# A scheduling planner gets measured lengths, a two-engine reservation and a new order of weight slabs

## The chip, the cores and the metric

The kernel runs on one core of one Trainium2 chip, in one launch. The metric is the device time in microseconds (us) of that core. Five engines share the work and run at their own pace: PE (TensorE: matmuls and transposes), DVE (VectorE), ACT (ScalarE), POOL (GpSimd) and SP (SyncE), whose queue issues every DMA of this kernel. Each engine carries out its own list of instructions in order. Semaphores hold an instruction back until what it reads has been written, and until what it overwrites has been read.

## The reference

One layer of a bidirectional encoder on 512 tokens of width 1024, all in float32:

```
h   = rms_norm(x)
all = h @ w_in          # attention q,k,v,gate az; delta q,k,v (dq,dk,dv), beta, decay, gate dz; merge gates gA,gB
A   = softmax(rope(norm(q)) rope(norm(k))^T / sqrt(128)) v          # 8 heads, 2 kv heads
y_att = (A * silu(az)) @ w_br_att
qkv = silu(short_conv(dq,dk,dv))                                    # depthwise, 5 taps
o   = gated delta rule over qkv, chunk by chunk, forward + backward  # needs (I + L)^-1 per chunk, head, direction
y_dn = (rms_norm(o) * silu(dz)) @ w_br_dn
mix = (sigmoid(gA) * y_att + sigmoid(gB) * y_dn) @ w_out
x   = x + rms_norm(mix)
x   = x + rms_norm(sigmoid(x @ w_ple_gate) * (p @ w_ple_proj))
```

## The kernel before, in words

**Products.** Each float32 product is made from three PE passes. A matrix is split into a rounded part `hi` and a rest `lo`, and lo x hi, hi x lo and hi x hi are added up in one PSUM bank (lines 434 to 436 in `gemm_t`, 451 to 453 in `gemm_n`, 469 to 471 in `gemm_k`). The weights come as *slabs* of 1024 x 128 (512 KB), 72 of them: dq, dk, dv, dz, az, gA, gB, ydn (the branch projection of the delta rule) and yatt (that of attention), eight each. A slab takes eight steps of three matmuls, 128 x 512. The other weights (kv, q0, q1, out0, out1, pg0, pg1) come in blocks of the same size in bytes. `fetch` (line 377) issues the DMA of each into one of two `wraw` buffers. `loader` (392) has `split` (192) make the two parts: ACT casts `whi`, and then DVE or POOL subtracts to give `wlo`.

**What hangs on a slab.** dq, dk and dv go through `conv_tail` (678): one ACT pass, four DVE taps that read PSUM, a tanh on ACT, a DVE product, four PE transposes, and one more DVE pass. The gates dz, az, gA and gB go through `gate_tail` (482): tanh on ACT, one DVE product for dz and az and none for gA and gB, and a DMA to DRAM, from where they are read back later.

**The delta rule** runs for two groups of four heads. `phase_a` (759) makes the masked products kk and qk, inverts 32 x 32 triangles on DVE and combines them to 128 x 128 on PE. The inversion is here called the *chain*: 30 steps that depend on one another, each of a product (833) and a subtraction (835), both with two operands in SBUF. `phase_b` (939) is the scan over chunks. Group 1 starts when group 0 has been scanned. `phase_y` (1041) normalises and gates the result. `att_head` (1261) does the attention of one head; `yatt_job` (1399), `out_job` (1477) and `pg_job` (1537) finish the layer.

**The planner.** The order of the instructions on every engine is made while the program is built, by `Flow` (line 33). Each part of the kernel is a generator. Flow keeps a clock `now`, and a list of busy intervals for each engine. `op` (66) finds the first free place of a given length on one engine and books it; all instructions are put out in the order of their planned starts. ("pe", cost) moves the clock on by the planned length of some matmuls. Nothing of these times reaches the chip: only the order does, and there the semaphores decide when each instruction starts. `V`, `A` and `G` (151 to 158) book DVE, ACT and POOL; `Q` (160) books the issue of a DMA, and so the order on SP's queue. `ORDER` (126) lists the slabs and blocks, `OUT0` tells before which slabs the four blocks of out0 are fetched, `PR` gives the priorities of parts (a lower number goes first), and `GAP` a pause between bursts of small matmuls. `split` puts the subtraction of a slab on POOL where that ends less than 1.5 us (of planned time) later than on DVE.

```
    def fit(self, eng, dur, t):                    # line 57
...
        while i < len(busy) and busy[i][0] < t + dur:
            t = max(t, busy[i][1])
...
        for m in range(30, 0, -1):                 # line 837, the chain
            t = V(0.25 + 2 * m * (31 - m) * 0.00108, t - 0.1, step, m)
```

Of the kernel before, what the change touches and what calls it, by code (L numbers as in the profile page):

```python
# [34 lines left out]
class Flow:  # L35
    """Interleaves the kernel's parts (generators) into one instruction order.

    A part yields ("pe", cost) behind matrix instructions, ("at", t) and ("ev", event) to wait,
    ("get", tag) to take a tile slot; the first part in priority that can go on is traced next.
    Instructions of the other engines are traced in the order of their planned starts.  # L40
    """
# [97 lines left out]
W1 = 0  # L139


@with_exitstack
def layer(ctx, tc, x, p, wt, wba, wn, wpp, npre, rows, qkn, hd16, npost, pnorm, dnorm, cs, out):
# [43 lines left out]
    def either(dep, *ways):  # L187
        """the way that ends first"""
        w = min((F.fit(w[0], w[1], max(F.now + 0.2, dep + 0.15))[0] + w[1], i, w) for i, w in enumerate(ways))[2]
        return op(w[0], w[1], dep, *w[2:])  # L190

    def split(src, hi, lo, dep, n, sbuf=False, slow=False):
# [8 lines left out]
        fn = (dve if eng == "DVE" else pool).tensor_sub  # L201
        t2 = op(eng, n * (0.00113 if eng == "DVE" else 0.00228), t, fn, lo, src, hi.bitcast(F32))
# [43 lines left out]
    def rsqrt(n, dep, s, mul, eps, post=1.0, src=None):  # L246
        """s = post (mul src + eps)^-1/2, n elements in each partition; src is s if not given"""
# [175 lines left out]
    def gemm_t(name, mh=hh, ml=hl, need=None):  # L423
        """need: events by k"""
# [6 lines left out]
        for k in range(8):  # L431
# [8 lines left out]
            yield "pe", 0.648  # L440
        return o

    def gemm_n(name, t, sh, sl_):
        yield "get", "mm"
        o = bank("mm")
        for k in range(8):
# [7 lines left out]
            yield "pe", 0.648  # L454
        return o

    def gemm_k(name, sh, sl_):
        """the four token tiles at once, so that the weights pass through"""
# [4 lines left out]
        for k in range(8):  # L463
            yield "ev", slab["blk", name, k // 2][0]
            hi, lo = (w[:, k % 2, :] for w in slab["blk", name, k // 2][1])
            for t in range(NT):
# [73 lines left out]
    # e^c, e^(clast - c), e^clast; each [dir, chunk, head]  # L540
# [1138 lines left out]
```

## Time and profile before

| | |
|---|---|
| median of 3 runs | 802.01 us (801.99 to 803.83) |
| the profiled execution: first to last instruction | 802.0 us |
| PE busy | 770.2 us, 96% |
| DVE busy | 517.7 us, 65% |
| POOL busy | 363.3 us, 45% |
| ACT busy | 316.8 us, 39% |
| mean granted clock of TensorE | 0.983 of full speed |
| DMA | 96.70 MB, mean 121 GB/s |

Busy time is the union of the intervals in which an engine had an instruction under way. The granted clock is given as a share of 2.4 GHz: 1.00 is 2.4 GHz and 0.50 is 1.2 GHz, and a value between them is a mean over a stretch that holds both. The span and the median agree, so that stretches of the trace can be set directly against the measured time. Many lines of the trace have the number L89: this is where Flow puts out booked instructions, so they are told apart by the names of their tiles.

### The profile page before, as it was taken

What the parts mean: (1) busy time and instruction counts of PE and PEld (TensorE: products, weight loads), DVE (VectorE), ACT (ScalarE), POOL (GpSimd) and SP (SyncE); (2) the same over time, 40 slices, a digit from 0 to 9 for tenths busy, and PEclk for the clock granted to TensorE, in tenths of its full rate; (3) what the DMA queues carried; (4) which work ended last, traced back from release to release, by engine and by line L of the source; (5) the groups of instructions that cost most, each with busy time, mean ns of one, the idle gap of its engine ahead of it and who ended that gap; (6) DMA issues with size and microseconds to landing.
All of it is one profiled execution on the core that took longest, in us unless ns stands there. A gap on an engine that the chain in (4) does not pass through costs nothing.

```text
span 802.0 us, 11761 instructions
## 1 busy us (share of the span) xinstructions
PE 770.2 (96%) x4522; PEld 636.1 (79%) x4522; DVE 517.7 (65%) x904; ACT 316.8 (39%) x522; POOL 363.3 (45%) x303
## 2 busy tenths in 40 slices
PE   8999999898999999996999999999999999989995
PEld 6787888686789987884779988887888888878884
DVE  4577788998845599996556554618677644523634
ACT  6465433325342144322434133424666533331421
POOL 6354574243521277443332116845465554461421
PEclk9999999998999999998899999999999999999999
DMA  6463226226211263525313116334144346643213
GB/s 247 131 198 107 79 92 158 84 87 158 66 55 40 92 197 115 150 92 153 130 54 105 40 53 190 104 120 132 66 157 132 119 141 217 225 137 133 87 45 131
DMA packets 52970, 96.70 MB, mean 121 GB/s; under 512 B 20849, under 2 KB 22449, under 8 KB 52914
## 3 DMA queue, kind: packets, MB, share of 16 engines
q1 hardware_dynamic: 52914, 95.95, 37.9%
q8 instruction: 35, 0.57, 0.3%
q14 instruction: 21, 0.17, 0.1%
HBM read 79.12 MB, written 16.81 MB: 120 GB/s over the span
## 4 chain that ended last, share of the span: by engine, by line
PE 73%; DVE 17%; DMA 3%; issue 2%; ACT 2%; POOL 2%; SPq 0%; POOLq 0%; DVEq 0%; ACTq 0%
PE mm L434 11%; PE mm L436 11%; PE mm L435 11%; DVE blk L835 4%; PE mm L451 4%; PE mm L452 4%; PE mm L453 4%; DVE u L89 3%; DVE f L89 3%; DVE blk L833 3%; PE mm L469 3%; PE mm L470 3%; PE mm L471 3%; PE aux L1007 2%; PE aux L975 2%
## 5 line engine op out<-in xcount | busy, mean ns | idle before, releaser
L89 POOL TENSOR_TENSOR wlo<-wraw,whi 128x1024 fp32r<-128x1024 f32 x71 | 170.5, 2402 | 259.9 <-ACT whi L89 241.8
L434 PE MATMUL mm<-u,wlo 128*128 128x512 f32 x576 | 236.5, 411 | 4.8 <-POOL wlo L89 4.6
L436 PE MATMUL mm<-u,whi 128*128 128x512 f32 x576 | 227.0, 394 | 0.0
L435 PE MATMUL mm<-u,whi 128*128 128x512 f32 x576 | 226.8, 394 | 0.0
L434 PEld LDWEIGHTS mm<-u,wlo 128*128 128x128 f32 x576 | 109.6, 190 | 26.6 <-POOL wlo L89 5.6
L436 PEld LDWEIGHTS mm<-u,whi 128*128 128x128 f32 x576 | 109.5, 190 | 24.1
L435 PEld LDWEIGHTS mm<-u,whi 128*128 128x128 f32 x576 | 109.9, 191 | 19.7
L89 ACT CAST whi<-wraw 128x1024 fp32r<-128x1024 f32 x84 | 87.9, 1046 | 67.9 <-PE mm L471 28.3
L89 DVE SCALAR_TENSOR_TENSOR f<-mm,cw,f 128x510 f32<-128x510 f32 (+1 forms) x96 | 71.7, 748 | 13.6 <-ACT f L89 10.9
L451 PE MATMUL mm<-u,u 128*128 128x512 f32 x128 | 51.4, 402 | 2.2 <-DVE u L89 2.2
L452 PE MATMUL mm<-u,u 128*128 128x512 f32 x128 | 50.6, 395 | 0.0
L453 PE MATMUL mm<-u,u 128*128 128x512 f32 x128 | 50.5, 395 | 0.0
L89 POOL TENSOR_TENSOR u<-wraw,u 128x1024 fp32r<-128x1024 f32 x15 | 36.6, 2440 | 27.7 <-ACT u L89 27.6
L89 ACT ACTIVATE f<-mm 128x512 f32<-128x512 f32 (+1 forms) x44 | 25.5, 580 | 46.7 <-PE mm L453 30.0
L469 PE MATMUL mm<-whi,u 128*128 128x512 f32 x96 | 39.8, 415 | 2.5 <-ACT whi L89 2.5
L89 ACT ACTIVATE go<-mm 128x512 f32<-128x512 f32 x32 | 19.2, 599 | 56.6 <-PE mm L436 33.2
L470 PE MATMUL mm<-wlo,u 128*128 128x512 f32 x96 | 38.6, 402 | 1.9 <-POOL wlo L89 1.9
L89 DVE TENSOR_TENSOR u<-aux,u 128x512 f32<-128x512 f32 (+1 forms) x48 | 31.9, 685 | 12.5 <-ACT u L89 10.1
L471 PE MATMUL mm<-whi,u 128*128 128x512 f32 x96 | 38.5, 401 | 0.0
L835 DVE TENSOR_TENSOR blk<-blk,blk 128x30 f32<-128x30 f32 (+14 forms) x60 | 37.0, 616 | 2.1
L89 ACT COPY c<-aux 128x512 f32<-128x512 f32 x18 | 10.6, 586 | 62.7 <-DVE f L89 39.6
L89 POOL TENSOR_TENSOR u<-f,u 128x512 fp32r<-128x512 f32 x16 | 22.4, 1402 | 19.1 <-ACT u L89 19.1
(254 smaller groups left out, 1332.9 us busy)
## 6 DMA issues: line engine op xcount, KB each, us to landing
wraw<-in_wt_dram SPq DMA_DIRECT2D x72, 512.0 KB, 3.5
wraw<-in_wn_dram SPq DMA_DIRECT2D x28, 512.0 KB, 4.1
u<-CI SPq DMA_DIRECT2D x16, 256.0 KB, 6.8
u<-in_x_dram SPq DMA_DIRECT2D x4, 512.0 KB, 8.7
eD<-c SPq DMA_DIRECT2D x8, 256.0 KB, 2.1
gate_gA<-go SPq DMA_DIRECT2D x8, 256.0 KB, 2.8
gate_dz<-go SPq DMA_DIRECT2D x8, 256.0 KB, 2.1
gate_gB<-go SPq DMA_DIRECT2D x8, 256.0 KB, 3.0
```

The source lines that it names most:

```text
L89: fn(*a, **k)
L434: pe.matmul(o, lo[:, k, :], mh(k), start=(k == 0), stop=False)
L435: pe.matmul(o, hi[:, k, :], ml(k), start=False, stop=False)
L436: pe.matmul(o, hi[:, k, :], mh(k), start=False, stop=(k == 7))
L451: pe.matmul(o, b, hi, start=(k == 0), stop=False)
L452: pe.matmul(o, a, lo, start=False, stop=False)
L453: pe.matmul(o, a, hi, start=False, stop=(k == 7))
L469: pe.matmul(o[t], b, hi, start=(k == 0), stop=False)
L470: pe.matmul(o[t], a, lo, start=False, stop=False)
L471: pe.matmul(o[t], a, hi, start=False, stop=(k == 7))
L833: dve.tensor_tensor(out=tt[:, 0:m, 0:31 - m], in0=b[:, 0:m, m:m + 1].to_broadcast(sh), in1=w[:, m:m + 1, m + 1:].to_broadcast(sh), op=ALU. ...
L835: dve.tensor_sub(w[:, 0:m, m + 1:], w[:, 0:m, m + 1:], tt[:, 0:m, 0:31 - m])
```

## The change

Lengths in the planner are replaced: the three matmuls of a step from 0.648 to 0.682, four 128-column products from 0.87 to 0.90, four scan operations on DVE from 0.92 to 1.05, a POOL subtraction from 0.00228 to 0.00232 us an element, and so on. A new booking `W` takes a place that is free on DVE and on POOL at once, and reserves both; the instruction itself still runs on DVE. W replaces V for DVE work with two operands in SBUF (the chain, the split on DVE, the SiLU product of the conv tail, the merge sums, the sandwich norm and others). While a chain is being planned (`chains[0]` above 0), `split` uses POOL only where that ends no later than DVE would (`HOT` = 0, else `COOL` = 1.5). ORDER, OUT0, PR and GAP are new. Because slabs now come in any order within their kind, jobs count their turns (`turn`) where they tested for the first or the last index. No computation, tile or buffer changes.

```diff
+    def slot(self, engs, dur, dep):
+        t = max(self.now + 0.2, dep + 0.15)
+        while True:
+            at = [self.fit(e, dur, t) for e in engs]
+            if all(a == t for a, _ in at):
+                return t, [i for _, i in at]
+            t = max(a for a, _ in at)
...
+    def W(dur, dep, fn, *a, **k):
+        return op(("DVE", "POOL"), dur, dep, fn, *a, **k)
...
-            tv = F.fit("DVE", n * 0.00113, t + 0.15)[0] + n * 0.00113
-            tp = F.fit("POOL", n * 0.00228, t + 0.15)[0] + n * 0.00228
-            if slow or tp < tv + 1.5:
+            eng = ("DVE", "POOL")
+            tv = F.slot(eng, n * 0.00113, t)[0] + n * 0.00113
+            tp = F.slot(("POOL",), n * 0.00232, t)[0] + n * 0.00232
+            if slow or tp < tv + (HOT if chains[0] else COOL):
                 eng = "POOL"
...
+        chains[0] += 1
         for m in range(30, 0, -1):
-            t = V(0.25 + 2 * m * (31 - m) * 0.00108, t - 0.1, step, m)
+            t = W(0.32 + 2 * m * (31 - m) * 0.00104, t - 0.1, step, m)
             yield "at", t - 1.0
+        chains[0] -= 1
...
-            yield "pe", 0.648
+            yield "pe", 0.682
...
 ORDER = """
-dq0 dk0 gA0 dq1 dk1 dq2 dk2 dk3 dq3 dk4 dz0 dq4 dk5 dq5 dz1 gA1
-dk6 dv0 gB0 gB1 dz2 dv1 dv2 dk7 dv3 dq6 gB2 dq7 az0 dz3 gA2 az1
-az2 dz4 gB3 dv4 dv5 dv6 az3 dz5 gB4 dz6 az4 gA3 dv7 az5 kv dz7
-gA4 gB5 gB6 gA5 az6 q0 gB7 ydn0 q1 gA6 az7 gA7 ydn1 free_h ydn2 ydn3
-ydn4 ydn5 ydn6 ydn7 vec yatt0 yatt1 yatt2 yatt3 yatt4 yatt5 yatt6 yatt7 out0 out1 pg0
+dq2 az3 dk3 dk0 dq3 dq0 dk1 dk2 dq1 dv0 dz2 gB1 dk7 dz4 dq7 dk6
+dz3 dz7 dz0 gB6 dz6 gA7 dk5 dv1 dv2 dv3 az2 dq6 dk4 dq5 dq4 az4
+gB4 gA5 dz1 dv7 dv6 gA6 az1 az0 dv5 gA4 gB7 gA1 gA0 az5 az6 dv4
+kv gA2 gA3 dz5 gB5 q0 az7 gB3 q1 ydn2 gB0 ydn6 gB2 free_h ydn3 ydn0
+ydn1 ydn5 ydn4 ydn7 yatt5 yatt6 vec yatt1 yatt4 yatt7 yatt2 yatt0 yatt3 out0 out1 pg0
 pg1
 """
-OUT0 = 'ydn3 ydn4 ydn5 yatt2'
-PR = dict(dec=9, dm1=7, y=2, conv=5, gate=9, kv=2, q=6, head=7, ple=11)
-GAP = 0.6
+OUT0 = 'ydn0 ydn4 ydn5 yatt6'
+PR = dict(dec=7, dm1=7, y=1, conv=3, gate=0, kv=5, q=7, head=1, ple=11)
+GAP = 0.0
+COOL, HOT = 1.5, 0
```

## Rows read from the trace of the kernel before

**Rows 1.** The page's first part: busy time, share of the span and number of instructions of PE, DVE and POOL.

```profile
PE 770.2 (96%) x4522; PEld 636.1 (79%) x4522; DVE 517.7 (65%) x904; ACT 316.8 (39%) x522; POOL 363.3 (45%) x303
```

**Rows 2.** The busy time of each engine by stage. Columns: the stretch in us from the start, its length, then PE, PEld (weight loads), DVE, ACT and POOL busy with their numbers of instructions, the granted clock, the share of the DMA engines, GB/s.

```profile
136.00:206.00 70.00, 63.00 (x416) 50.01 (x415) 63.22 (x105) 27.09 (x39) 25.90 (x12) 0.93 0.39 116
206.00:300.00 94.00, 93.97 (x759) 80.64 (x759) 59.40 (x122) 31.04 (x49) 37.04 (x30) 1.00 0.29 91
300.00:390.00 90.00, 80.52 (x427) 65.46 (x426) 79.06 (x127) 32.73 (x45) 43.47 (x27) 0.94 0.44 131
540.00:698.00 158.00, 157.45 (x765) 130.78 (x765) 101.00 (x191) 79.09 (x141) 83.74 (x70) 1.00 0.45 147
698.00:716.00 18.00, 15.79 (x63) 12.54 (x62) 7.61 (x7) 6.56 (x9) 10.85 (x6) 0.91 0.46 141
```

**Rows 3.** The same view for the five stretches in which TensorE had the lower granted clock behind an idle time of PE.

```profile
153.60:157.00 3.40, 3.40 (x10) 2.65 (x9) 3.26 (x6) 1.43 (x4) 2.40 (x1) 0.50 0.02 5
184.30:191.10 6.80, 5.31 (x15) 4.34 (x16) 4.21 (x6) 5.27 (x9) 2.38 (x1) 0.50 1.03 203
368.60:372.00 3.40, 3.40 (x8) 2.69 (x9) 3.02 (x13) 0.00 (x0) 0.38 (x1) 0.50 0.00 0
378.80:385.70 6.90, 4.98 (x13) 3.87 (x13) 4.60 (x7) 5.76 (x10) 1.92 (x1) 0.51 0.90 234
706.50:709.90 3.40, 3.40 (x10) 2.62 (x9) 0.60 (x1) 1.63 (x3) 2.97 (x2) 0.50 0.22 58
```

**Rows 4.** What PE waited for: us in total, how often, the longest.

```profile
PE mm L434 <- POOL wlo L89: 4.6, 2, 3.3
PE mm L666 <- DVE f L89: 3.5, 1, 3.5
PE mm L666 <- DVE u L89: 3.5, 2, 3.0
```

**Rows 5.** The timeline of POOL and of DVE in the first chain: start, duration, engine, line, operation, tiles and shapes; x4 is four instructions in one row.

```profile
138.66 2.40 POOL L89 TENSOR_TENSOR wlo<-wraw,whi 128x1024 fp32r<-128x1024 f32 x1 [3.62 <-ACT whi L89]
153.72 2.40 POOL L89 TENSOR_TENSOR wlo<-wraw,whi 128x1024 fp32r<-128x1024 f32 x1 [7.09 <-ACT whi L89]
...
138.79 2.34 DVE L833 TENSOR_TENSOR blk<-blk,blk 128x58 f32<-128x58 f32 x1
141.17 0.22 DVE L835 TENSOR_TENSOR blk<-blk,blk 128x58 f32<-128x58 f32 x1
...
153.49 3.10 DVE L89 SCALAR_TENSOR_TENSOR f<-mm,cw,f 128x510 f32<-128x510 f32 x4
```

**Rows 6.** The two chains whole (138.3 to 181.3, 335.0 to 371.8), all engines; then the products of the chain (line 833) and its subtractions (line 835) alone, DVE only, in stretches that hold one chain each.

```profile
138.30:181.30 43.00, 39.97 (x174) 32.68 (x173) 40.59 (x75) 11.99 (x17) 17.08 (x8) 0.96 0.26 89
335.00:371.80 36.80, 33.54 (x143) 27.33 (x142) 34.93 (x67) 8.37 (x11) 14.40 (x7) 0.96 0.28 93
...
136.00:184.00 48.00, 13.46 (x30) 0.96 0.32 106
333.00:373.00 40.00, 13.89 (x30) 0.96 0.27 92
...
136.00:184.00 48.00, 18.52 (x30) 0.96 0.32 106
333.00:373.00 40.00, 18.45 (x30) 0.96 0.27 92
```

**Rows 7.** Groups of instructions: engine, operation, tiles, shapes, number | busy us, mean ns of one | idle time before them. POOL's slab subtractions in the stretches 136 to 184 and 333 to 373, and the same subtraction where DVE did it, over the whole run.

```profile
L89 POOL TENSOR_TENSOR wlo<-wraw,whi 128x1024 fp32r<-128x1024 f32 x7 | 16.9, 2413 | 27.7 <-ACT whi L89 27.7
L89 POOL TENSOR_TENSOR wlo<-wraw,whi 128x1024 fp32r<-128x1024 f32 x6 | 14.6, 2432 | 23.8 <-ACT whi L89 23.8
...
L89 DVE TENSOR_TENSOR wlo<-wraw,whi 128x1024 fp32r<-128x1024 f32 x13 | 17.9, 1373 | 2.0 <-ACT whi L89 1.2 <-POOL u L89 0.8
```

**Rows 8.** The timeline of DVE and of SP's queue at the end of the second chain (SPq is the queue that issues DMAs, in order), and ACT's cast of the slab behind them.

```profile
360.52 0.68 DVE L89 SCALAR_TENSOR_TENSOR go<-go,mm 128x512 f32<-128x512 f32 x1
361.23 0.32 SPq L89 DMA_DIRECT2D gate_dz<-go  x1
361.64 0.38 SPq L89 DMA_DIRECT2D wraw<-in_wt_dram  x1
365.00 1.04 ACT L89 CAST whi<-wraw 128x1024 fp32r<-128x1024 f32 x1 [0.87 <-DMA wraw<-in_wt_dram]
371.81 0.32 SPq L89 DMA_DIRECT2D dW<-blk  x1
372.23 0.37 SPq L89 DMA_DIRECT2D wraw<-in_wn_dram  x1
```

**Rows 9.** The timeline around the start of out0: PE's first matmul of it, the first of its second step, the last one ahead of the wait and the one behind it; then the merge sum on DVE beside a subtraction on POOL.

```profile
698.57 0.39 PE L451 MATMUL mm<-u,u 128*128 128x512 f32 x1
699.25 0.39 PE L451 MATMUL mm<-u,u 128*128 128x512 f32 x1
703.10 0.39 PE L453 MATMUL mm<-u,u 128*128 128x512 f32 x1
705.71 0.50 PE L451 MATMUL mm<-u,u 128*128 128x512 f32 x1 [2.21 <-DVE u L89]
...
701.66 2.60 DVE L89 TENSOR_TENSOR gi<-gi,go 128x512 f32<-128x512 f32 x1
701.33 2.39 POOL L89 TENSOR_TENSOR u<-wraw,u 128x1024 fp32r<-128x1024 f32 x1 [2.23 <-ACT u L89]
```

More of the change, by code (lines that the diff above doesn't have):

```diff
@@ L64, in fit @@
         return t, i
+    def slot(self, engs, dur, dep):
[5 more added lines that the diff above has]
+            t = max(a for a, _ in at)
     def op(self, eng, dur, dep, fn, *a, **k):
-        t, i = self.fit(eng, dur, max(self.now + 0.2, dep + 0.15))
-        self.eng[eng].insert(i, (t, t + dur))
+        engs = eng if isinstance(eng, tuple) else (eng,)
+        t, at = self.slot(engs, dur, dep)
+        for e, i in zip(engs, at):
+            self.eng[e].insert(i, (t, t + dur))
         if fn is not None:
@@ L190, in either @@
         return op(w[0], w[1], dep, *w[2:])
+    chains = [0]
     def split(src, hi, lo, dep, n, sbuf=False, slow=False):
@@ L196, in split @@
         if sbuf:
-            tv = F.fit("DVE", n * 0.00113, t + 0.15)[0] + n * 0.00113
-            tp = F.fit("POOL", n * 0.00228, t + 0.15)[0] + n * 0.00228
-            if slow or tp < tv + 1.5:
+            eng = ("DVE", "POOL")
+            tv = F.slot(eng, n * 0.00113, t)[0] + n * 0.00113
+            tp = F.slot(("POOL",), n * 0.00232, t)[0] + n * 0.00232
+            if slow or tp < tv + (HOT if chains[0] else COOL):
                 eng = "POOL"
-        fn = (dve if eng == "DVE" else pool).tensor_sub
-        t2 = op(eng, n * (0.00113 if eng == "DVE" else 0.00228), t, fn, lo, src, hi.bitcast(F32))
+        fn = (pool if eng == "POOL" else dve).tensor_sub
+        t2 = op(eng, n * (0.00232 if eng == "POOL" else 0.00113), t, fn, lo, src, hi.bitcast(F32))
         return t, t2
@@ L659, in conv_silu2 @@
         t2 = A(0.52, t, act.activation, dst, y, AF.Tanh, scale=0.5)
-        return V(0.67, t2, dve.scalar_tensor_tensor, out=dst, in0=dst, scalar=1.0, in1=y, op0=ALU.add, op1=ALU.mult)
+        return W(0.62, t2, dve.scalar_tensor_tensor, out=dst, in0=dst, scalar=1.0, in1=y, op0=ALU.add, op1=ALU.mult)
     def transposed(src):
@@ L728, in layer, with turn @@
     conv_ready = {(k, g): Event() for k in ("dk", "dq", "dv") for g in range(2)}
+    begun = {}
+    def turn(key):
+        begun[key] = begun.get(key, -1) + 1
+        return begun[key]
     def conv_job(kind, hd):
-        g, h = hd // 4, hd % 4
-        if h == 0:
+        g = hd // 4
+        nth = turn((kind, g))
+        if nth == 0:
             u = {"dk": (4, 7), "dq": (5, 8), "dv": (10, 10)}[kind][g]
@@ L827, in phase_a @@
         yield "at", t - 0.5
[L828 to L829 removed]
+        t = W(0.65, t, dve.tensor_scalar, out=w, in0=b, scalar1=-1.0, scalar2=None, op0=ALU.mult)
+        t = W(0.15, t, dve.memset, w.rearrange("p a b -> p (a b)")[:, 0:1024:33], 1.0)
         def step(m):
@@ L998, in phase_b @@
                 else:
-                    tS = heads(0.92, 0.0, lambda h, pS=pS, c=c: dve.scalar_tensor_tensor(
+                    tS = heads(1.05, 0.0, lambda h, pS=pS, c=c: dve.scalar_tensor_tensor(
                         out=st8[:, h, :], in0=st8[:, h, :], scalar=ex[:, 2, d, c, 4 * g + h:4 * g + h + 1],
@@ L1015, in phase_b @@
             if s > 0:
-                t = heads(0.92, t, lambda h, oq=oq, c=c: dve.scalar_tensor_tensor(
+                t = heads(1.05, t, lambda h, oq=oq, c=c: dve.scalar_tensor_tensor(
                     out=o[:, c, h, :], in0=oq[:, h, :], scalar=ex[:, 0, d, c, 4 * g + h:4 * g + h + 1],
@@ L1344, in att_head @@
         free("f2", t)
-        if h == 3:
-            free("u9")
-            free("u10")
-        if h == 7:
-            for u in (11, 12, 6, 15):
+        if turn(("head", b)) == 3:
+            for u in ((9, 10), (11, 12))[b]:
+                free(f"u{u}")
+        if turn("head") == 7:
+            for u in (6, 15):
                 free(f"u{u}")
@@ L1393, in yatt_tail @@
         t = A(0.55, t, act.mul, hi, th, 0.5)
-        t = V(0.68, t, dve.scalar_tensor_tensor, out=lo, in0=th, scalar=0.5, in1=hi.bitcast(F32),
+        t = W(0.68, t, dve.scalar_tensor_tensor, out=lo, in0=th, scalar=0.5, in1=hi.bitcast(F32),
               op0=ALU.mult, op1=ALU.subtract)
@@ L1460, in out1_tail @@
             hs = slice(half * 512, half * 512 + 512)
-            tr = V(0.68, tr, dve.scalar_tensor_tensor, out=xa[:, hs], in0=src, scalar=rs, in1=xa[:, hs],
+            tr = W(0.68, tr, dve.scalar_tensor_tensor, out=xa[:, hs], in0=src, scalar=rs, in1=xa[:, hs],
                    op0=ALU.mult, op1=ALU.add)
@@ L1512, in pg_tail @@
         z = late["z0"][:, t, :] if half == 0 else th
-        tz = V(0.68, max(ta, te), dve.scalar_tensor_tensor, out=z, in0=th, scalar=1.0, in1=e, op0=ALU.add, op1=ALU.mult)
+        tz = W(0.68, max(ta, te), dve.scalar_tensor_tensor, out=z, in0=th, scalar=1.0, in1=e, op0=ALU.add, op1=ALU.mult)
         free("go", tz)
@@ L1519, in pg_tail @@
         yield "ev", need
-        tz = V(0.62, ts, dve.tensor_mul, z, z, late["pno"][:, half * 512:half * 512 + 512])
+        tz = W(0.62, ts, dve.tensor_mul, z, z, late["pno"][:, half * 512:half * 512 + 512])
         if half == 0:
@@ L1611, in layer @@
                 places["blk", nm] = a[1]
-    for i, w in enumerate(OUT0.split()):
+    before = sorted(((w[:-1], int(w[-1])) for w in OUT0.split()), key=names.index)
+    for i, w in enumerate(before):
         names.remove(("blk", "out0", i))
-        names.insert(names.index((w[:-1], int(w[-1]))), ("blk", "out0", i))
+        names.insert(names.index(w), ("blk", "out0", i))
     for n in names:
```

69 lines of the change are left out of this document (33 added, 36 removed).

## The prediction

> **What bounds the kernel now.** I read the page's first part, then the busy time by stage, then what PE waited for, and last the timelines around each wait.
>
> The first part says PE: 770.2 us of 802.0 are busy, DVE has 517.7 and POOL 363.3 [rows 1]. PE's work is nearly the same before and after the change, so the question is only how much of PE's lost time comes back. The stages show where it is lost [rows 2]. Between 136 and 206 PE is busy 63.00 of 70 us, and between 300 and 390 it is busy 80.52 of 90: 7.0 and 9.5 us of idle time. From 206 to 300 and from 540 to 698 the idle time is 0.03 and 0.55 us. The reader should see that the two losing stages are those in which DVE is nearly full (63.22 of 70, 79.06 of 90), and that they hold the two chains (138.3 to 181.3 and 335.0 to 371.8 [rows 6]). A third place is the start of out0: 2.2 us [rows 2, 9].
>
> An idle PE costs twice. Behind the gaps the granted clock is 0.50, that is 1.2 GHz, for 23.9 us in five pieces [rows 3]. PE is busy 3.40 + 5.31 + 3.40 + 4.98 = 17.1 us in the four pieces of the two chain stages; at 2.4 GHz that work takes half, so 8.5 us are lost there, and 1.7 in the piece behind out0's wait. Not every gap pays this: the first wait of 1.3 us for `wlo` near 63 us (4.6 less 3.3 [rows 4]) has no slow piece behind it in rows 3.
>
> So the two chain stages lose 7.0 + 9.5 + 8.5 = 25.0 us, out0's start 2.2 + 1.7 = 3.9, the first wait 1.3. Everything else is PE at work, the start and the last tile, which the change does not touch.
>
> **Why DVE is late there.** A step of the chain whose twin takes 0.22 us took 2.34 [rows 5]. It began at 138.79, just behind a POOL subtraction (138.66, 2.40 long), and ended when POOL ended. Four conv taps, which have one operand in PSUM, took 3.10 us together, 0.78 each, across the whole POOL subtraction of 153.72; none of them was held. So POOL holds up DVE work with two SBUF operands and not the rest, which is the rule that the change gives the planner. The price: the chains took 13.46 + 18.52 = 32.0 and 13.89 + 18.45 = 32.3 us of DVE time [rows 6]. Six steps in each were held up by some 2.05 us, so that 12.3 us of each are waiting and 19.7 to 20.0 work. The old plan booked 30 x 0.25 + 2 x 4960 x 0.00108 = 18.2 us for a chain (4960 is the sum of m (31 - m)), and no waiting.
>
> From there each large gap can be followed. The transposes of line 666 waited up to 3.0 and 3.5 us for DVE's conv tails [rows 4], which stand behind held-up steps in DVE's list. In the second chain the lateness goes round by SP's queue [rows 8]: DVE's gate product starts at 360.52, the store of the gate waits for it and issues at 361.23, the next slab's load stands behind the store and issues at 361.64, and ACT's cast waits for it until 365.00. That is the wait of 3.3 us for `wlo`. The same happens once more at 371.81, where the chain's own store goes ahead of the load of a kv block (372.23). Both are a queue made for a chain 12 us shorter than the real one.
>
> **The change part by part.**
>
> *Chain lengths and W.* A chain is now booked at 30 x 0.32 + 2 x 4960 x 0.00104 = 19.9 us, with POOL reserved beside it. That agrees with the 19.7 to 20.0 above. Splits are booked between the steps, and with HOT = 0 they go to DVE unless POOL ends no later. In the chain stretches POOL made 7 and 6 of them, 16.9 and 14.6 us [rows 7]. On DVE one takes 1.37 as a mean, which holds some waiting. If all 13 move, DVE gains 13 x 1.37 = 17.8 us of work and loses 24.6 of waiting: 6.8 us net. If all stay on POOL, each still keeps the chain out for about 2.1 us, which is nothing gained. I take the first, since it is what the booking chooses when both engines are free. What counts more is that the rest of the plan, SP's queue with it, is now made for the real length.
>
> *The order of slabs.* While the first chain ran, the old order had dk6 dv0 gB0 gB1 dz2 dv1 dv2 dk7 in work (the 17th to the 24th slab), five of them conv slabs. The same places now hold dz3 dz7 dz0 gB6 dz6 gA7 dk5 dv1, with two. A conv slab costs DVE four taps (3.10 [rows 5]) and two more passes of about the gate product's 0.68 [rows 8], some 4.5 us; a gate 0.7 or nothing. So three conv slabs, some 13 us of DVE work, leave the first chain. They come back behind it (dk5 dv1 dv2 dv3 az2 dq6 dk4 dq5 dq4), where the scan leaves DVE busy only 59.40 of 94 us [rows 2]. In the second chain one conv slab stood among seven before, and one or two stand there now. Taken together the first chain should end some 10 to 15 us sooner, the second some 5 to 8.
>
> *PE lengths.* A step is booked at 0.682 where it was 0.648; rows 9 show 699.25 - 698.57 = 0.68. There are 576 steps of gemm_t and 288 others of this form, so the old plan's PE ran 864 x 0.034 = 29 us fast. This removes nothing by itself. It takes away 0.034 us of slack a step that other engines had without booking it: bounds from 0 to a rival below. I take 0 here and count new waits in the sum.
>
> *GAP, PR, turns, the other lengths.* The bursts of small matmuls follow one another at once; PE work stays the same, and the total of each priority change lies between nothing and one wait of the size in rows 4. I take nothing.
>
> *The end of yatt.* out0 adds over eight k-steps and step k needs mix k. Before, yatt7 came last, so seven steps (4.78 us, 698.57 to 703.3) ran before the wait. The new order ends with yatt0 and yatt3, so only three steps (2.04) can run ahead of mix 3. The tail from yatt's end to the next matmul took 705.71 - 698.57 = 7.1 us, of which 1.9 are a merge sum held up by POOL (2.60 against some 0.7). The wait becomes 7.1 - 2.0 = 5.1 if the sum is still held up, and 3.2 if W prevents it: 1.0 to 2.9 us more than now. I take 1.5.
>
> **The sum.** 802.0 - 25.0 (chain stages) - 1.3 (first wait) + 1.5 (out0) = 777.2. A plan this tight will have waits of its own. One of 2.2 us with its slow piece costs 3.9, as at out0; I count two, rounded down to 7 in all: 784.2. The span and the median agree (802.0, 802.01), so **784 us**, 2.2% less. Its own range is 777 to 793: none of the new waits, or four.
>
> **Rivals.**
>
> *The waiting is moved, not removed.* A booked place makes no instruction faster. If splits stay on POOL the first chain's stretch needs 19.7 + 16.9 = 36.6 us in which one of the two engines must stand aside, and the second 20.0 + 14.6. Then about half of the 25.0 comes back: 802 - 12.5 + 1.5 + 3.9, or 795. For it: POOL did 13 of these splits. Against: HOT sends them to DVE. Beside this, the Trainium skill (SBUF — State Buffer, section SBUF: two separate sides) says that the shared ports are an exclusive lock that the first comer keeps for its whole instruction. By that rule the plan can only choose who waits, which is this rival; the trace agrees that it is a full block (2.34 against 0.22).
>
> *The plan does not hold on the chip.* Only order is fixed; when times drift by a microsecond, a POOL split lands on a chain step again. Then the twelve stretched steps stay and only the lighter slab order helps. The time is 800 to 804. For it: the split waits for a DMA (rows 8), whose time the planner books as before. Against: booked gaps are made by order, and order on one engine holds.
>
> *Slower: the slack is gone where heads run.* The place is 540 to 698, where eight attention heads pass their work from PE to DVE, ACT, POOL and back, and PE now idles 0.55 us. If the 29 us of unbooked slack were what hid those hand-overs, each head would wait once or twice; at 3.9 us a wait the gain of 25 is gone from the seventh wait on, and eight heads with one wait each give 777 + 8 x 3.9 = 808. For it: all lengths are now booked without reserve, and heads rise from priority 7 to 1. Against: DVE is busy 101 of 158 us there, POOL 84, so a wait is more likely to be hidden.
>
> **Chances.** Forecast 0.56, waiting moved 0.18, plan does not hold 0.09, slower 0.17. A difference under 0.3%, 2.4 us, cannot be told from no change. The first two cases are faster, as is a little of the third; most of the third is no change: faster 0.75, same 0.08, slower 0.17. The range of 8 in 10 goes from 772 (everything found, and the out0 wait too) to 805.
>
> **What would show it.** Right: lines 833 and 835 sum to 40 to 46 us over the two chains where they had 64.3; more than 13 slab subtractions on DVE; PE's idle time in the chain stages under 5 us; fewer pieces at clock 0.50. The out0 step is right if the wait comes behind nine matmuls and is longer than 2.2. Wrong: steps of over 2 us still in the chain, or idle time of PE among the heads.

## The result and the profile after

The change made the kernel slower by under half a per cent: 806.52 us (median of 7 runs, 805.07 to 807.06) against 802.24 (7 runs), a ratio of 1.0036 with a 95% interval of 1.0022 to 1.0049. The forecast was 784. The profiled execution has a span of 804.9 us. The lines of the code have moved by 12 to 30: 434 is now 454, 451 is 471, 666 is 686, 800 and 805 are 828 and 833, the chain's 833 and 835 are 861 and 863, and Flow's L89 is L101.

The page's first part after the change, against [rows 1]:

```profile
PE 764.8 (95%) x4522; PEld 634.8 (79%) x4522; DVE 485.5 (60%) x902; ACT 316.4 (39%) x522; POOL 354.0 (44%) x305
```

PE is busy 5.4 us less, but 40.1 us idle (804.9 - 764.8) where it was 31.8. DVE lost 32 us of busy time and two instructions (x904 to x902): most of it (24.6 us) is waiting that stood in stretched chain steps. The chain's two lines show it. Below are line 861 (the first two rows) and line 863 on DVE, one chain in each stretch; the last columns are clock, DMA share and GB/s:

```profile
120.00:210.00 90.00, 9.87 (x30) 1.00 0.46 134
325.00:400.00 75.00, 9.87 (x30) 1.00 0.57 162
...
120.00:210.00 90.00, 9.97 (x30) 1.00 0.46 134
325.00:400.00 75.00, 9.97 (x30) 1.00 0.57 162
```

The two chains take 39.7 us where they took 64.3 [rows 6]. No step is held up any more. The slab subtractions in the stretches of [rows 7], first 136 to 184, then 333 to 373, and then the subtraction on DVE over the whole run:

```profile
L101 DVE TENSOR_TENSOR wlo<-wraw,whi 128x1024 fp32r<-128x1024 f32 x7 | 8.6, 1222 | 0.9 <-ACT whi L101 0.9
L101 POOL TENSOR_TENSOR wlo<-wraw,whi 128x1024 fp32r<-128x1024 f32 x2 | 4.8, 2408 | 48.8 <-ACT whi L101 47.6 <-issue 1.2
...
L101 DVE TENSOR_TENSOR wlo<-wraw,whi 128x1024 fp32r<-128x1024 f32 x6 | 7.3, 1222 | 0.1
L101 POOL TENSOR_TENSOR wlo<-wraw,whi 128x1024 fp32r<-128x1024 f32 x2 | 4.8, 2401 | 6.3 <-ACT whi L101 6.3
...
L101 DVE TENSOR_TENSOR wlo<-wraw,whi 128x1024 fp32r<-128x1024 f32 x14 | 17.1, 1222 | 1.1 <-ACT whi L101 0.9
```

Read these together. DVE now makes 14 splits of this form, and all 14 lie in the chains: the 14th runs at 133.7, ahead of the stretches shown, but behind the first chain's start at 132.7. Before, it made 13, all of them outside the chains. So outside the chains its share fell from 13 to none, and POOL, which takes twice as long for one (2.40 against 1.22 us), does the rest. A second form, with tiles named `u` (the 16 blocks of out and pg and two of the embedding), went the same way: DVE made 3 of 18 before, and none after.

The busy time by stage, after, in the columns of [rows 2], four of whose stretches come first; the last three are the places of the new losses:

```profile
136.00:206.00 70.00, 69.20 (x586) 56.63 (x586) 60.84 (x113) 29.94 (x43) 11.80 (x7) 1.00 0.41 128
300.00:390.00 90.00, 81.78 (x381) 67.98 (x379) 66.12 (x127) 32.39 (x47) 38.23 (x30) 0.96 0.50 143
540.00:698.00 158.00, 155.33 (x752) 127.94 (x750) 93.25 (x183) 77.40 (x138) 91.35 (x75) 1.00 0.45 148
698.00:716.00 18.00, 13.22 (x50) 10.16 (x49) 8.17 (x6) 6.97 (x9) 11.85 (x7) 0.81 0.46 142
...
280.00:330.00 50.00, 41.36 (x220) 35.18 (x219) 35.99 (x58) 18.15 (x28) 34.77 (x30) 0.93 0.47 127
330.00:400.00 70.00, 67.61 (x545) 55.49 (x544) 46.28 (x96) 24.20 (x33) 19.38 (x13) 1.00 0.54 159
470.00:560.00 90.00, 81.31 (x366) 64.89 (x365) 50.18 (x74) 29.38 (x44) 57.16 (x53) 0.98 0.35 113
```

The same three of the kernel before:

```profile
280.00:330.00 50.00, 48.34 (x259) 41.18 (x258) 46.54 (x63) 21.68 (x32) 37.12 (x29) 1.00 0.55 157
330.00:400.00 70.00, 62.17 (x495) 48.28 (x494) 52.34 (x91) 21.48 (x29) 25.64 (x17) 0.93 0.42 127
470.00:560.00 90.00, 89.45 (x424) 73.57 (x422) 47.18 (x80) 32.30 (x47) 51.14 (x48) 1.00 0.40 126
```

Both chain stages are nearly full again (69.20 of 70 and 67.61 of 70 us). But PE lost 7.0 us between 280 and 330, where the second group's masked products begin, and 8.1 between 470 and 560, where the delta rule's output is normalised. What PE waited for after the change (us in total, times, longest), against [rows 4]:

```profile
PE aux L833 <- DVE u L101: 6.5, 2, 5.9
PE mm L454 <- POOL wlo L101: 5.6, 4, 2.0
PE mm L471 <- DVE u L101: 4.8, 1, 4.8
PE mm L1095 <- DVE u L101: 3.5, 4, 1.1
PE mm L1250 <- DVE f L101: 2.5, 2, 1.4
```

Of the old list the two waits of line 666 are gone (0.9 us is left at line 686), and line 454 has four short waits for POOL's splits in place of two. Of the others, two were there and grew: line 833 (805 before, 1.7 us) and line 471 (451 before, 2.2 us [rows 9]). Line 1095 is new, and line 1250 (1220 before) had 0.3 us. The stretches with the lower clock are now four, against five in [rows 3]:

```profile
65.30:68.70 3.40, 3.40 (x12) 2.72 (x11) 2.84 (x5) 0.64 (x2) 2.16 (x1) 0.50 0.56 166
307.70:314.50 6.80, 3.92 (x17) 3.66 (x18) 4.90 (x8) 0.81 (x1) 6.80 (x8) 0.50 0.00 0
485.20:488.60 3.40, 3.40 (x12) 2.69 (x10) 0.26 (x1) 0.62 (x1) 3.40 (x3) 0.50 0.29 77
700.20:707.00 6.80, 3.97 (x9) 2.81 (x9) 5.70 (x4) 2.67 (x4) 4.59 (x2) 0.50 0.51 151
```

Each of the four large gaps has its slow piece; two waits of 1.4 and 1.2 us near 550 have none. The timelines show what stands behind the three largest: the second group's masks, the norm (with the shortest, median and longest of its four passes in ns), and the start of out0, which answers to [rows 9]:

```profile
295.04 2.35 POOL L101 TENSOR_TENSOR wlo<-wraw,whi 128x1024 fp32r<-128x1024 f32 x1
304.55 1.28 DVE L101 TENSOR_TENSOR u<-u,cj 128x512 f32<-128x512 f32 x2
306.88 7.02 POOL L101 TENSOR_TENSOR u<-u,Nj 128x512 f32<-128x512 f32 x7
310.02 2.08 PE L833 MATMUL aux<-u,u 128*128 128x128 f32 x8 [5.92 <-DVE u L101]
...
477.96 2.38 POOL L101 TENSOR_TENSOR wlo<-wraw,whi 128x1024 fp32r<-128x1024 f32 x1
478.03 6.25 DVE L101 TENSOR_TENSOR u<-u,kinv 128x512 f32<-128x512 f32 x4 [3.97 <-POOL kinv L101]
480.30 4.58 POOL L101 TENSOR_TENSOR u<-f,f 128x256 f32<-128x256 f32 x4
L101 DVE TENSOR_TENSOR u<-u,kinv x4: 1207/1209/2857, 478.0 to 483.1; 128x512 f32<-128x512 f32 x4
...
696.77 2.37 POOL L101 TENSOR_TENSOR u<-wraw,u 128x1024 fp32r<-128x1024 f32 x1 [2.33 <-ACT u L101]
697.13 2.55 DVE L101 TENSOR_TENSOR gi<-gi,go 128x512 f32<-128x512 f32 x1
697.86 0.39 PE L456 MATMUL mm<-u,whi 128*128 128x512 f32 x1
700.08 2.34 POOL L101 TENSOR_TENSOR u<-wraw,u 128x1024 fp32r<-128x1024 f32 x1 [0.95 <-ACT u L101]
700.57 2.40 DVE L101 SCALAR_TENSOR_TENSOR u<-gi,u 128x512 fp32r<-128x512 f32 x1 [0.89 <-ACT u L101]
703.03 0.79 PE L471 MATMUL mm<-u,u 128*128 128x512 f32 x1 [4.78 <-DVE u L101]
```

At 304.55 the last two decay additions of the second group begin, where the last one had ended by 300.9 before; POOL's products behind them start at 306.88, and PE waits until 310.02. At 478 a norm that W had reserved ran beside a POOL split all the same: its first pass took 2.86 us, and the other three, beside four smaller POOL products, 1.21 each; undisturbed, such a pass takes 0.68. At 697 a merge sum took 2.55 us, and at 700 the subtraction that makes the `lo` of the same tile took 2.40, each beside a POOL split of an out block. So outside the chains W did not keep the two engines apart. A reserved place has no instruction in POOL's list, so POOL does not stop for it: the split began at 477.96, just as POOL's own last step for the norm ended. In the chains no split ran beside a step because DVE makes all 14 itself; e12 below shows what happens when POOL makes them.

### The profile page after: what moved, and what is told of

Read it like the earlier page. It is cut to its first block, busy times and chain, and to the rows that moved or that the text cites. A ratio compares the mean times of both kernels' runs of the same rounds, so it can differ in the third digit from the quotient of the medians.

```text
span 804.9 us, 11746 instructions
## 1 busy us (share of the span) xinstructions
PE 764.8 (95%) x4522; PEld 634.8 (79%) x4522; DVE 485.5 (60%) x902; ACT 316.4 (39%) x522; POOL 354.0 (44%) x305
## 4 chain that ended last, share of the span: by engine, by line
PE 75%; DVE 9%; DMA 5%; POOL 4%; issue 3%; ACT 3%; SPq 0%; POOLq 0%; DVEq 0%; ACTq 0%
PE mm L454 12%; PE mm L456 12%; PE mm L455 12%; PE mm L471 4%; PE mm L473 4%; PE mm L472 4%; DVE f L101 4%; PE mm L489 2%; PE mm L491 2%; PE mm L490 2%; DVE u L101 2%; POOL u L101 2%; PE mm L1339 2%; PE aux L1005 2%; PE aux L1037 2%
## 5 line engine op out<-in xcount | busy, mean ns | idle before, releaser
L101 POOL TENSOR_TENSOR wlo<-wraw,whi 128x1024 fp32r<-128x1024 f32 x70 | 168.1, 2403 | 294.7 <-ACT whi L101 291.1
L454 PE MATMUL mm<-u,wlo 128*128 128x512 f32 x576 | 233.5, 405 | 5.6 <-POOL wlo L101 5.6
L101 ACT CAST whi<-wraw 128x1024 fp32r<-128x1024 f32 x84 | 88.2, 1050 | 165.2 <-PE mm L456 106.4
L456 PEld LDWEIGHTS mm<-u,whi 128*128 128x128 f32 x576 | 108.4, 188 | 23.7
L455 PEld LDWEIGHTS mm<-u,whi 128*128 128x128 f32 x576 | 108.8, 189 | 19.6
L101 DVE SCALAR_TENSOR_TENSOR f<-mm,cw,f 128x510 f32<-128x510 f32 (+1 forms) x96 | 71.9, 748 | 23.5 <-ACT f L101 21.0
L101 POOL TENSOR_TENSOR u<-wraw,u 128x1024 fp32r<-128x1024 f32 x18 | 44.4, 2474 | 16.3 <-ACT u L101 16.1
L101 DVE TENSOR_TENSOR u<-aux,u 128x512 f32<-128x512 f32 (+1 forms) x48 | 32.0, 688 | 22.7 <-ACT u L101 12.5
L101 ACT ACTIVATE f<-mm 128x512 f32<-128x512 f32 (+1 forms) x44 | 24.8, 579 | 48.6 <-PE mm L473 39.9
L471 PEld LDWEIGHTS mm<-u,u 128*128 128x128 f32 x128 | 24.4, 191 | 10.6 <-DVE u L101 5.8
L101 ACT COPY c<-aux 128x512 f32<-128x512 f32 x18 | 10.7, 592 | 49.9 <-DVE f L101 23.2
L101 DVE TENSOR_TENSOR blk<-mm,blk 128x512 fp32r<-128x512 f32 x32 | 21.2, 687 | 12.9 <-ACT blk L101 12.9
L473 PEld LDWEIGHTS mm<-u,u 128*128 128x128 f32 x128 | 24.4, 191 | 5.4
```

What stands on the lines that cost most here:

```text
L101: fn(*a, **k)
L454: pe.matmul(o, lo[:, k, :], mh(k), start=(k == 0), stop=False)
L455: pe.matmul(o, hi[:, k, :], ml(k), start=False, stop=False)
L456: pe.matmul(o, hi[:, k, :], mh(k), start=False, stop=(k == 7))
L471: pe.matmul(o, b, hi, start=(k == 0), stop=False)
L473: pe.matmul(o, a, hi, start=False, stop=(k == 7))
```

## The experiments

All ratios are to the kernel before, timed beside the run on the same chip. e4 became the base of most of them.

**Is it the order or the planner?** Three runs take them apart. e1 is the changed kernel with the old ORDER, OUT0, PR and GAP. e2 has the new order with the old lengths and no reservation, and e3 adds the new lengths to it:

```diff
# e2 and e3
-COOL, HOT = 1.5, 0
+COOL, HOT = 1.5, 1.5
...
 def W(dur, dep, fn, *a, **k):
-    return op(("DVE", "POOL"), dur, dep, fn, *a, **k)
+    return op("DVE", dur, dep, fn, *a, **k)
...
-            eng = ("DVE", "POOL")
+            eng = ("DVE",)
```

> The changed kernel with ORDER, OUT0, PR and GAP of the kernel before; the new lengths, W and HOT stay. Two theories. ORDER: the new rule is a gain and the new slab order and priorities bring the new waits. It expects the chain stages to be as full as in the changed kernel and the new waits (303, 480, 698 us) to be gone: 785 to 795 us. RULE: the reservation itself makes the plan, and so PE's list, wait where DVE and POOL work is booked one behind the other, and the new order only makes up for that. It expects slower than the changed kernel: 810 to 825 us.

> The changed kernel with the old lengths, W booking DVE alone and HOT = COOL; the new ORDER, OUT0, PR and GAP stay. ORDER expects the new waits to stay and the held-up chain steps to come back on top: 812 to 825 us. RULE expects the new waits at 303 and 480 us to go while chain steps are held up again, at a time near or under the kernel before: 790 to 802 us.

> The changed kernel with the new lengths and the new order, but W books DVE alone and HOT = COOL: only the reservation is gone. RULE expects most of the new waits to go and only some chain steps held up: 785 to 800 us. ORDER expects the waits to stay, and the chain to be held up: 806 to 820 us. If the lengths alone had made the new waits by taking the slack away, this would be as slow as the changed kernel with the chain at fault nowhere.

Measured: e1 828.81 us (ratio 1.033, 1.0288 to 1.0371), e2 818.0 (1.019, 1.0157 to 1.0222), e3 811.92 (1.0118, 1.0089 to 1.0146). The stage 136 to 206, of e1 and then of e2:

```profile
136.00:206.00 70.00, 70.00 (x324) 57.86 (x323) 63.29 (x119) 25.94 (x37) 7.73 (x9) 1.00 0.39 124
```

```profile
136.00:206.00 70.00, 55.73 (x482) 45.05 (x480) 56.11 (x97) 24.55 (x36) 24.01 (x12) 0.88 0.38 113
```

The first chain's stage comes back by the new planner even with the old order, and is worse than before with the new order alone (55.73 against 63.00 [rows 2]). Chain steps of over 1.5 us are gone in e1, and stay in e2 and e3, six in the first chain and five in the second of each. So W and HOT together, and neither the lighter slabs nor the new lengths, freed the chains. e1 is above both ranges that were named for it; e2 and e3 lie in those of ORDER. Either half alone makes the kernel slower. With the new order, W and HOT as a whole are still a gain: e3, without them, is 5 us slower than the change.

**The same on the old kernel.** e6 puts only the chain's real lengths, its reservation and HOT = 0 into the kernel before; e7 only the new lengths.

> The kernel before (old order, priorities, GAP and lengths) with one thing added: a chain step is booked at its real length on DVE and POOL together, and splits in a chain with HOT = 0. SPREAD expects the 25 us of the chain stages to come back in part: 785 to 798 us. FIT expects 806 to 825 us, with the chain steps no longer held up and new waits of PE behind it.

> The kernel before with the new lengths alone: old order, priorities and GAP, W books DVE alone, HOT = COOL. It splits the 26 us that the whole new planner cost the old order (e1). FIT expects 808 to 816 us, some half of it. If the reservation alone did it, 800 to 804 us.

Measured: e6 825.15 us (1.0278, 1.0246 to 1.0309), e7 818.59 (1.0195, 1.0162 to 1.0227). In e6 no chain step is held up. Parts of the new planner, with an order that was not made for it, cost 16 to 22 us.

**The start of out0.** e4 leaves everything as in the change but lets yatt0 to yatt7 come in rising order:

```diff
-ydn1 ydn5 ydn4 ydn7 yatt5 yatt6 vec yatt1 yatt4 yatt7 yatt2 yatt0 yatt3 out0 out1 pg0
+ydn1 ydn5 ydn4 ydn7 yatt0 yatt1 vec yatt2 yatt3 yatt4 yatt5 yatt6 yatt7 out0 out1 pg0
-OUT0 = 'ydn0 ydn4 ydn5 yatt6'
+OUT0 = 'ydn0 ydn4 ydn5 yatt1'
```

> The changed kernel with yatt0 to yatt7 in rising order again (out0's third block is fetched ahead of yatt1, the same place). Both theories: out0 now has seven steps to run ahead of its wait and not none to three; the wait goes from 4.9 us to between 1 and 4, and with the slow piece behind it 2.7 to 4 us are gained: 802 to 804 us. If the end of yatt is held up by something that does not depend on the order, 806 as the changed kernel.

Measured: 803.74 us (1.0019, 1.0001 to 1.0036), 2.8 less than the change, but 1.4 by the ratios, whose intervals overlap: a small gain at most. PE's waits at line 471 come to 4.0 us where they were 4.8. As far as the traces name instructions, by line, tile and shape, every engine of e4 has the same list as the changed kernel; only which yatt slab comes when is different.

**The reservation inside the chain and outside.** e5 is e4 with POOL reserved for the chain's steps, and for splits made while a chain is planned, alone. R is the old W:

```diff
 def W(dur, dep, fn, *a, **k):
-    return op(("DVE", "POOL"), dur, dep, fn, *a, **k)
+    return op("DVE", dur, dep, fn, *a, **k)
...
-            eng = ("DVE", "POOL")
+            eng = ("DVE", "POOL") if chains[0] else ("DVE",)
...
-            t = W(0.32 + 2 * m * (31 - m) * 0.00104, t - 0.1, step, m)
+            t = R(0.32 + 2 * m * (31 - m) * 0.00104, t - 0.1, step, m)
```

> e4_yatt_in_order with the reservation of both engines kept for the chain's steps and for the splits made while a chain is planned; all other W book DVE alone. Two theories are left. SPREAD: the reservation gains in the chain and costs elsewhere (the waits at 305 and 480 us). It expects the waits at 305 and 480 to shrink and the chain stages to stay full: 792 to 800 us. FIT: an order and the planner it was found with only work as a pair, and any other planner for the same order puts waits into PE's list at new places. It expects slower than e4: 806 to 815 us.

Measured: **789.86 us** (0.9833, 0.98 to 0.9865), 14 us less than e4. In e5:

```profile
280.00:330.00 50.00, 47.30 (x249) 40.32 (x248) 42.78 (x61) 20.60 (x32) 35.86 (x29) 0.97 0.51 142
470.00:560.00 90.00, 87.19 (x415) 70.75 (x414) 52.38 (x95) 36.03 (x59) 53.07 (x51) 1.00 0.32 110
```

Both new losses are nearly gone, while the stage 136 to 206 stays at 69.19 of 70 us. So SPREAD is right, with more gain than it named, and FIT, which expected a loss from any other planner, is refuted. Booking both engines for all the rest costs more than it gives. e12 takes HOT out of e5 (HOT = 1.5).

> e5_chain_only with HOT = COOL, so that splits in a chain go to POOL whenever they end less than 1.5 us later there. If putting them on DVE is what the chain stage lives on, the chains grow by some 2 us for each split moved back and this is 794 to 800 us. If the true length and the reservation suffice, 788 to 792 us.

Measured: 796.83 us (0.993, 0.9905 to 0.9954). Sending splits to DVE during the chain is worth some 7 us. e12 shows more. POOL is still reserved beside every chain step, but it makes 17 splits while the chains run, and 14 steps are held up again, seven in each chain; the chains' two lines take 67.9 us, where the change has 39.7. One of them:

```profile
149.87 2.39 POOL L101 TENSOR_TENSOR wlo<-wraw,whi 128x1024 fp32r<-128x1024 f32 x1 [3.53 <-ACT whi L101]
149.91 2.58 DVE L865 TENSOR_TENSOR blk<-blk,blk 128x210 f32<-128x210 f32 x1
```

So the reservation alone does not protect the chain. HOT does, by leaving POOL without splits there. (It can hold: in e6 the four POOL splits inside the chains ran beside conv taps and not beside steps.) What HOT would do without the chain's reservation, which makes POOL look busy to `split`, was not run.

**Which use outside the chain?** Four guesses on single causes: in e8 dz1 changes places with dz6, because its gate was stored late for the second group; in e9 the eight decay additions of phase_a go on V in e4; e10 puts them back on R in e5; e11 reserves, in e4, DVE work only against POOL's streaming instructions, and not against its powers, selects and memsets (nor the small scalings in the same helper as a power).

> e4_yatt_in_order with dz1 and dz6 changed for each other in ORDER, two gates of the same work. In the changed kernel SP's queue stood 5.8 us for the store of gate dz1, which is read back at once, with slab loads and DVE's next work behind it, just ahead of the longest wait (6.1 us at 304). If that is its cause the wait shrinks to 1 to 3 us: 797 to 801 us. If the wait is made by POOL and DVE taking turns over the decay tiles, the queue's wait goes and PE's stays: 802 to 805 us.

> e4_yatt_in_order with one use of W taken back: the eight additions to the decay tiles in phase_a book DVE alone. e5, which takes back all but the chain's, was 14 us faster than e4. If the wait at 305 us and what it delays behind it (group 1's chain, scan and norm) is the larger part, this is 793 to 798 us, with the first addition near 288 and not 294 us. If the cost is spread over the many other uses, 800 to 804 us.

> e5_chain_only with the eight additions reserved on both engines again, the complement of e9. With the first reading of e9 this gives back the larger part of the gain: 795 to 800 us. With the second it stays at 789 to 793 us.

> e4_yatt_in_order with a weaker rule: W excludes POOL's streaming work (subtractions, products, tensor_scalar) but not its powers, selects and fills. In e5 a decay addition took 0.69 us beside a power of 2.93 us on POOL, so the full rule books waits that the chip does not have. If that excess is what costs, this is 789 to 796 us with W everywhere. If any reservation outside the chain costs, 800 to 804 us.

Measured: e8 804.06 us (1.0016, 1.0 to 1.0031), nothing. e9 801.19 (1.0009, 0.9983 to 1.0035) and e10 791.5 (0.9862, 0.9841 to 0.9883): by the ratios to e4 and e5 the additions weigh 1 to 2 us, and the intervals overlap. e11 795.53 (0.9911, 0.9885 to 0.9936): a weaker exclusion gives 8 us, and leaves open for which instructions.

The splits were left. e13 is e4 with one line changed, and e14 is its complement: e5 with the old line put back.

```diff
# e13
-            eng = ("DVE", "POOL")
+            eng = ("DVE", "POOL") if chains[0] else ("DVE",)
```

> e4 with one use of the reservation taken out: outside a chain, a slab split on DVE is booked on DVE alone (it had to find DVE and POOL free at once). Every other reservation of e4 stays. Theory 1: the split's reservation is the main part of the 14 us between e4 (803.7) and e5 (789.9), since a place free on both engines comes late, and so the split goes to POOL, where it takes 2.4 us instead of 1.2, and the matmuls get their slab late. Then 788 to 796 us, with 25 or more splits on DVE (e4 has 14, e5 has 32). Rival 2: the cost is the reservation of the other DVE work (powers and decay additions, conv products, norms). Then 801 to 805, and the splits may go to DVE without a gain. Rival 3: both in parts, 796 to 801.

> The complement of e13: e5 (reservation for the chain only, 789.9 us) with the split's reservation put back everywhere, all other DVE work outside the chain still booked on DVE alone. Theory 1 (the split's reservation is the main part of the 14 us): 797 to 804 us, with some 14 splits on DVE. Rival 2 (the other DVE work): 788 to 792. Rival 3 (both in parts): 792 to 797.

Measured: e13 **783.95 us** (0.9761, 0.9745 to 0.9777), e14 799.42 (0.9945, 0.9921 to 0.9969). Taken out of e4, the split's reservation gives 20 us, more than Theory 1 named, and put into e5 it costs 9.5. That the two differ suggests that what it costs depends on what else is reserved. In e13:

```profile
136.00:206.00 70.00, 68.74 (x566) 56.16 (x566) 61.29 (x115) 28.43 (x41) 13.76 (x7) 1.00 0.39 122
280.00:330.00 50.00, 45.54 (x232) 38.17 (x231) 42.98 (x62) 19.18 (x30) 27.74 (x25) 0.93 0.47 150
470.00:560.00 90.00, 89.28 (x432) 73.53 (x431) 52.15 (x100) 38.34 (x65) 53.01 (x51) 1.00 0.33 113
```

```profile
PE mm L454 <- DVE wlo L101: 4.3, 1, 4.3
```

```profile
L101 DVE TENSOR_TENSOR wlo<-wraw,whi 128x1024 fp32r<-128x1024 f32 x26 | 33.5, 1288 | 4.1 <-ACT whi L101 3.7
L101 DVE TENSOR_TENSOR u<-wraw,u 128x1024 fp32r<-128x1024 f32 x9 | 16.7, 1856 | 9.9 <-ACT u L101 9.9
```

DVE makes 26 splits of the first form: 13 in the chains, and 13 outside, as before the change. They take 1.29 us as a mean, so they are hardly held up, though POOL is not kept clear for them. It also makes nine of the second form, which the kernel before left to POOL but for three; these are held up (1.86 us as a mean). One large wait is left (4.3 us, for a split on DVE), the wait of line 833 is gone, and the norm's stage is full. Without that line the other reservations outside the chain are a gain: e13 is 5.9 us under e5, which lacks them.

e15 and e16 ask how it acts, in e4: e15 lets the choice of engine look at DVE alone but still books both, e16 chooses as e4 does and books DVE alone.

```diff
# e15
-            tv = F.slot(eng, n * 0.00113, t)[0] + n * 0.00113
+            tv = F.slot(eng if chains[0] else ("DVE",), n * 0.00113, t)[0] + n * 0.00113
# e16, a line added behind it
+            eng = eng if chains[0] else ("DVE",)
```

> e4 (803.7 us) with only the choice between DVE and POOL changed for slab splits outside a chain: it compares POOL's end with the end on DVE alone, as e13 does; a split that then goes to DVE is still booked with POOL reserved. Theory 1a (the 20 us between e4 and e13 come from the choice: splits sent to POOL take 2.4 us instead of 1.2 and use up POOL): most of the gain stays, 784 to 792 us, with 22 or more splits on DVE. Theory 1b (they come from the booking: a split that needs both engines gets a late place and shuts POOL): under a third of it, 798 to 804. Between them: both.

> The other half: e4 with the choice for slab splits made as in e4, from the end of a place free on both engines, and a split that goes to DVE then booked on DVE alone. Theory 1a (choice): 799 to 804 us, with some 14 to 16 splits on DVE. Theory 1b (booking): 784 to 794, still with few splits on DVE.

Measured: e15 800.33 us (0.9969, 0.995 to 0.9989), e16 803.94 (1.0015, 0.9998 to 1.0031). Neither half gives the gain alone. e16 is no test of the booking: all 14 of its splits on DVE lie in the chains, as in e4, so no split was left to book more freely, and its lists are those of e4. e15 has 30 of the first form on DVE (and six of the second), but outside the chains with both engines booked for each, and PE waits elsewhere:

```profile
PE aux L833 <- DVE u L101: 9.0, 2, 8.1
PE mm L490 <- DVE wlo L101: 3.9, 1, 3.9
```

So it isn't the number of splits on DVE by itself. Shown is that the free choice alone gives 3 to 4 us of the 20, and that the rest comes only when the booking is free too. That a reserved split either goes to the slow engine or shuts the other for its time, so that the plan behind it is late either way, is my reading of the two.

**Luck of one list?** An edit can make the whole list of instructions anew. e17 and e18 repeat e13 and e5 with the unrelated swap of e8.

> Control: e13 (split free outside a chain, 783.95 us) with dz1 and dz6 swapped in the order, the small edit that moved e4 by 0.3 us in e8. Any edit makes the whole list of instructions anew, so a gain can be the luck of one list. If the 20 us belong to the split's booking, this stays within 4 us of e13: 780 to 788. If they are luck of that list, it lands anywhere between e13 and e4: 790 to 804.

> The same control on e5 (reservation for the chain only, 789.9 us), with dz1 and dz6 swapped. If the gain over e4 belongs to the booking: 786 to 794. If it is luck of one list: 795 to 804.

Measured: e17 782.61 us (0.975, 0.9726 to 0.9774), e18 788.83 (0.9825, 0.9796 to 0.9853), 1.3 and 1.0 us from their twins. e13 and e17 beat both kernels by over 18 us. But the swap did not do what it was meant for: as far as the traces name instructions, the lists of e17, e18 and e8 are, on every engine, those of e13, e5 and e4. So these runs show that the times repeat, and say nothing on luck. The other runs say more. The new order with HOT = 0 and the chain's reservation has four different lists in which a split outside the chains books both engines (e4, e9, e14, e15) and three in which it books one (e5, e10, e13). The four take 799.4 to 803.7 us and the three 784.0 to 791.5; e11, with its weaker rule, lies between. That makes luck unlikely for this order; with another order the booking was not tried.

## Why the prediction was wrong

The forecast's sum, with what the trace shows for each term (in us; idle time, and half of PE's time in a slow piece). The chain stages are taken as 136 to 206 and 330 to 400, since the new wait at 304 falls into the forecast's 300 to 390:

| term | forecast | measured |
|---|---|---|
| chain stages | -25.0 | 69.20 - 63.00 = 6.2; 67.61 - 62.17 = 5.4; four slow pieces gone, 8.5: **-20.1** |
| first wait | -1.3 | 0.7 more idle time between 20 and 136 (114.67 busy before, 113.96 after), a new slow piece 1.7: **+2.4** |
| out0 | +1.5 | wait 4.8 for 2.2, slow piece 2.0 for 1.7: **+2.9** |
| new waits | +7 | 280 to 330: 7.0 + 2.0; 470 to 560: 8.1 + 1.7: **+18.8** |
| sum | 784.2 | **806.0** (span 804.9, median 806.5) |

The table leaves out 1.6 us more idle time elsewhere and 2.7 us less work of PE at full clock, which make up the difference to the span.

**Right: the price of the held-up steps and its cause.** The chains' 64.3 us fell to 39.7, where 40 to 46 were to show it. PE idles 0.8 and 2.4 us in the two stages of the table, under the 5 named, and four fifths of the 25.0 came back; in the forecast's own stretch 300 to 390 it still idles 8.2 of the 9.5 us, so that this sign holds only once the new wait is counted by itself. The splits of the chains moved to DVE at 1.22 each, cheaper than the 1.37 taken. What freed the steps was this move; the reservation, to which the text gave the gain together with it, left 14 steps held up in e12.

**Right in direction, by another way: out0.** The wait is longer, 4.8 us, but it does not come behind nine matmuls: none of out0 runs ahead of it. The first matmul of out0, at 703.03, is the one that waits. Its step 0 needs mix 0, and yatt0 now comes last but one; the text looked only at mix 3. The sums were still held up, as for the text's 5.1 us, but that number had three steps run ahead, and that it is near 4.8 is luck.

**The step that failed: "W" was priced in the chain alone, and the "two" new waits were a count without a place.** The reservation also stands in the split, and the same line of `split` decides for all 84 slabs and blocks of the first form and the 18 of the second. The text followed it into 13 of them, and wrote that "DVE gains 13 x 1.37 = 17.8 us of work". DVE did gain 14 in the chains, but outside them it lost all 13, and the three of the second form. The term of 7 us for new waits measured 18.8, and e13 shows how much of the loss hangs on this one line: with it freed, and only the yatt order changed besides, the time is 783.95 us. How a reserved split makes PE wait where it does, at 304 and 481, was not shown. I looked for lost slack among the heads (540 to 698), from unbooked matmul time; PE idled 2.7 us there, all of it before 560, and was busy for all of 560 to 680 (120.00 of 120 us), so that rival's place was wrong though its sign was right.

**Wrong as well: the slab order.** Three conv slabs fewer in the first chain were to make it end 10 to 15 us sooner, and the second 5 to 8. The first runs from 132.7 to 175.4 (138.3 to 181.3 before): 6 us sooner, nearly all of it from its earlier start, and as long as it was. The second ends at 375.0, which is 3 us later. e2, with that order alone, leaves PE less busy in the first stage than before.

**The rivals.** "The waiting is moved, not removed" had this outcome in its name, but put it in the chain, where splits would stay on POOL. It moved to other stages. "The plan does not hold" is right for the norm at 478 and for out0's tile at 697, and for the chains of e12; in the changed kernel's chains it was not put to the test, as POOL has no split there. Its counter-argument, that order on one engine holds, says nothing on two engines. That 784 is the time of e13 is chance: it is another kernel, with the yatt slabs in order and the splits free. Its trace has much of the forecast's picture: full chain stages, one wait of 4.3 us that ends at 303, and one of 1.0 at out0.

## What to carry to other kernels

A conflict that the traces show can still be a bad constraint for a planner. Take the conflicting work off the second engine while a dependent chain runs, as HOT does, and leave work free that can go to either engine; a reserved place in a plan does not hold an engine back on the chip. When a helper's booking changes, count its calls in every stage and price each stage; a gain found where one looked says nothing on the others. Price an order and its planner apart: here either half alone was slower, and yet a third planner (e5, e13) was faster with the new order than the one that came with it. And before a run is taken as a control, see whether its lists differ from its twin's at all.

## What the runs showed of the hardware

POOL does not always hold up DVE work with two SBUF operands. In e5 a decay addition ran inside a POOL power (first POOL, then DVE):

```profile
287.73 2.93 POOL L268 TENSOR_TENSOR kinv<-kinv,pw 128x16 f32<-128x16 f32 x1
```

```profile
288.03 0.69 DVE L101 TENSOR_TENSOR u<-u,cj 128x512 f32<-128x512 f32 x1 [1.04 <-DMA u<-CI]
```

It took 0.69 us, as its undisturbed twins do (0.68), and ended nearly 2 us ahead of the power. The kernel before has the same: an addition of 0.68 us at 288.54, inside a power that ran 2.93 us from 287.39. The Trainium skill (SBUF — State Buffer, section SBUF: two separate sides) says that whichever of the two starts first gets the ports for its whole instruction and the other fully blocks. That agrees with POOL's 1024-element subtractions, beside which a chain step took 2.34 us [rows 5] and a merge sum 2.55, but not with this row, and the measurement decides. The 8 us that e11 gave fit this: a plan that keeps DVE off such POOL work pays for a conflict that does not come. Which of the three kinds of POOL work gave them was not tried.
